# Two attention jobs of one head pair each become one job: scores of the lower and the upper 64 partitions alternate on TensorE

## The chip, the cores and the metric

The kernel runs on one core of one Trainium2 chip. The metric is device time in microseconds (us) of one launch; below it is better. TensorE (PE) does the matmuls, PEld is its weight load, VectorE is DVE, ScalarE is ACT, GpSimd is POOL, SyncE is SP.

## The reference

256 tokens of width 1024 go through four layers of a first block and two layers of a second one. A layer of the first block projects x to queries, keys and values, attends, adds an attention over 256 memory rows, projects out, normalises, and runs a gated feed-forward of width 2816. The attention differs by layer: 12 heads of 64 with a top-k mask picked by an index of 8 small heads (layers 0 and 3), 4 value heads that share three dilated score groups (layer 1), 12 plain causal heads (layer 2). A layer of the second block has three branches: differential attention (4 heads, two score maps of 64 each, the second subtracted), latent attention (8 heads whose scores contract over 96), and sliding-window attention (8 query heads on 2 key heads of 64).

```
logits = jnp.einsum('bqhd,bqkhd->bhqk', qb, ks) * scale      # d = 64
p = softmax(where(valid, logits, -inf))
o = jnp.einsum('bhqk,bqkhd->bqhd', p, vs)
```

## The kernel before

**Tiling.** The tokens are two tiles of 128, t = 0 and t = 1, each worked by a generator of its own (`stream(t)`). Nearly all of TensorE's work is in the weight matmuls of `gemm_part` (L375 to L377): a float32 weight is split into a high part H (ACT, L330) and a rest L (DVE, L331), and three matmuls with up to 512 columns make one product. These are called weight matmuls below, and six of them (two weight tiles) are a unit. The two streams take turns, a unit or so at a time.

**Jobs.** Attention is cut into stages that a queue per stream (`defer`, `job`, `tick`) releases one tick, that is one unit, after the other: stage a computes the scores and the softmax, stage b transposes the probabilities (`p_T`), stage c multiplies by the values (`pv`) and normalises. `attend_job` makes one such job from two heads; the jobs of a stream start one tick apart. Within an engine the recorded instructions are put in order by a list scheduler, so the code's order is not quite the engine's.

**Halves.** Transposed queries and keys hold two heads in one block of 128 partitions, one in the lower 64 (0 to 63) and one in the upper 64. A job takes two heads of the same half (`half_slice(e)`), so a group of four heads gives two jobs, e = 0 with the lower half and e = 1 with the upper half. The scores are plain float32 with 64 contraction rows; the profile shows each such matmul as two passes on PE. The heads of 96 rows use no halves.

**PSUM.** Scores, transposed probabilities and value products all take a bank from the pool tag "w" of their stream, which has two banks; the weight matmuls have two banks per stream of their own ("mm").

**Around it.** In `index_jobs`, `group(g)` is run for g = 0 to 3, two groups a tick, one for each half. `dilated_job(h)` computes three score groups of one head in one stage. `diff_job` computes the map of the lower half in one stage, that of the upper half in the next.

Of the kernel before, what the change touches and what calls it, by code (L numbers as in the profile page):

```python
# [14 lines left out]
AF = mybir.ActivationFunctionType  # L15
ALU = mybir.AluOpType
# [49 lines left out]
def tile_two_blocks(  # L66
# [277 lines left out]
    def job(t, *stages):  # L344
        at = max(now[t] + 1, started[t] + 1)
        started[t] = at
        for k, fn in enumerate(stages):
            defer(t, fn, at=at + k)
        return at + len(stages)
# [117 lines left out]
    def scores(t, qs, kss):  # L467
        s = psum([P, 2, 256], "w")
        for j, (q, ks) in enumerate(zip(qs, kss)):
            for n, k in enumerate(ks):  # L470
                w = k.shape[1]
                pe.matmul(s[:, j, n * P : n * P + w], q, k, start=True, stop=True)
        return s

    def soft_pair(t, nk, qs, kss, biases, sums, inits=None, mins=None):
        s = scores(t, qs, kss)
        sm = work_tile([P, 2, nk], "sm", 2)
        n = len(qs)
        mn = mins if mins is not None else small(2, "mn")
# [162 lines left out]
    def attend_job(t, nk, qs, kss, biases, vs, done, after=None, **kw):  # L642
        st = {}

        def a():
            st["sums"] = kw.get("sums", None) if "sums" in kw else small(2, "sums")
            st["sm"] = soft_pair(t, nk, qs, kss, biases() if callable(biases) else biases, st["sums"],
                                 inits=kw.get("inits"), mins=kw.get("mins"))

        def b():  # L650
            st["pt"] = p_T(st["sm"], len(qs), nk)

        def c():
            done(pv(st["pt"], len(qs), nk, vs), st["sums"])

        return job(t, a, b, c)

# [1 line left out]
    def block1(t):  # L659
# [6 lines left out]
        for i in range(DEPTH):  # L666
# [20 lines left out]
            def head_jobs(g, mk):  # L687
                for e in range(2):
                    hs = [g + e, g + 2 + e]
                    r = half_slice(e)  # L690
                    end = attend_job(
                        t, nk, [qT[r, h // 2, :] for h in hs], [[k[r, h // 2, :] for k in kTs] for h in hs], [mk, mk],
                        [[w[:, h * 64 : h * 64 + 64] for w in vs] for h in hs],
                        lambda o, sums, e=e: normalise(by_parity(mix, g, e), o, sums, 2, 64))
                return end

            def mem_jobs():
                def one(e):
                    r = half_slice(e)

                    def ks():
                        return [[mem_kv[i][r, 0, b, :]] for b in range(2)]

                    kv = mem_kv[i]
                    return attend_job(
                        t, 256, [qmT[r, b, :] for b in range(2)], ks(), None,
                        [[kv[:, 1, kt, c : c + 64] for kt in range(2)] for c in (64 * e, 128 + 64 * e)],
                        lambda o, sums: normalise(by_parity(mix[:, 768:1024], 0, e), o, sums, 2, 64))

                one(0)  # L710
                return one(1)

            def dilated_job(h):
                st = {}
                e = half_slice(h % 2)
                rsum = []

                def a():
                    sm = work_tile([P, 3, nk], "sm", 2)
                    mn = small(3, "mn3")  # L720
                    rsum.append(small(1, "rsum"))
                    pss = []
                    for grp in ((0, 1), (2,)):
                        bl = [(4 * g + h) // 2 for g in grp]
                        pss.append(scores(t, [qT[e, b, :] for b in bl], [[k[e, b, :] for k in kTs] for b in bl]))
                    for g in range(3):
                        vec.tensor_tensor_reduce(
                            out=sm[:, g], in0=pss[g // 2][:, g % 2, :nk], in1=shared["dil"][:, g, moff:], scale=1.0,
                            scalar=3.0e38 if g == 0 else mn[:, g - 1 : g],
                            op0=ALU.add, op1=ALU.min, accum_out=mn[:, g : g + 1])  # L730
                    act.activation(sm, sm, AF.Exp, bias=mn[:, 2:3], scale=-1.0, accum_out=rsum[0])
                    vec.tensor_tensor(out=sm[:, 1], in0=sm[:, 1], in1=sm[:, 2], op=ALU.add)
                    vec.tensor_tensor(out=sm[:, 0], in0=sm[:, 0], in1=sm[:, 1], op=ALU.add)
                    st["sm"] = sm

                def b():
                    st["pt"] = p_T(st["sm"], 1, nk)

                def c():
                    o = pv(st["pt"], 1, nk, [[w[:, h * 192 : h * 192 + 192] for w in vs]])  # L740
                    normalise(mix[:, h * 192 : h * 192 + 192].unsqueeze(1), o, rsum[0], 1, 192)

                return job(t, a, b, c)

            def index_jobs(wi):
                def group(g):
                    r = half_slice(g % 2)
                    hs = [4 * (g // 2) + g % 2, 4 * (g // 2) + 2 + g % 2]
                    s = scores(t, [qiT[r, h // 2, :] for h in hs], [[k[r, :] for k in kiTs]] * 2)
                    rl = work_tile([P, 2, nk], "sm", 2)  # L750
                    act.activation(rl, s[:, :, :nk], AF.Relu)
                    for e, h in enumerate(hs):
                        if h == 0:
                            vec.tensor_scalar(score[:, :nk], rl[:, e], wi[:, 0:1], None, op0=ALU.mult)
                        else:
                            vec.scalar_tensor_tensor(out=score[:, :nk], in0=rl[:, e], scalar=wi[:, h : h + 1],
                                                     in1=score[:, :nk], op0=ALU.mult, op1=ALU.add)
# [14 lines left out]
                for g in range(4):  # L772
                    defer(t, lambda g=g: group(g), after=IDX_WAIT + 1 + g // 2)
# [59 lines left out]
            if kind == 1:  # L833
                for s in range(2):
# [7 lines left out]
                    for h in (2 * s, 2 * s + 1):  # L842
                        end = dilated_job(h)
                    ends.append(end)
# [65 lines left out]
    def block2(t):  # L910
# [4 lines left out]
        for l in range(DEPTH_2):  # L915
# [86 lines left out]
            for h in range(0, 8, 2):  # L1002
                mk = causal[:, moff:]
                end_b = attend_job(
                    t, nk, [mqT[:96, h + e, :] for e in range(2)],
                    [[s[0][:96, h + e, :] for s in sh] for e in range(2)], [mk, mk],
                    [[s[1][:, (h + e) * 64 : (h + e) * 64 + 64] for s in sh] for e in range(2)],
                    lambda o, sums, h=h: normalise(ob[:, h * 64 : h * 64 + 128].rearrange("p (h d) -> p h d", d=64),
                                                   o, sums, 2, 64))
# [5 lines left out]
            def diff_job(h0):  # L1015
                st = {}

                def a(m):
                    r = slice(64 * m, 64 * m + 64)
                    if m == 0:  # L1020
                        st["bias"] = load_bias(t, h0)
                        st["sums"] = small(4, "sums4")
                    st[m] = soft_pair(t, nk, [aqT[r, h0 + e, :] for e in range(2)],
                                      [[s[2][r, h0 + e, :] for s in sh] for e in range(2)],
                                      [st["bias"][:, e, :] for e in range(2)], st["sums"][:, 2 * m : 2 * m + 2])
                    if m == 0:
                        return
# [18 lines left out]
                end = job(t, lambda: a(0), lambda: a(1), b, c)  # L1046
                started[t] += 1
                return end
# [13 lines left out]
            for g in range(2):  # L1062
# [6 lines left out]

                for e in range(2):  # L1070
# [3 lines left out]
                    end_c = attend_job(  # L1074
                        t, nk, [cqT[r, h // 2, :] for h in hs], [[s[4][r, g, :] for s in sh]] * 2,
                        lambda e=e, f=bias_of: f(e), [[s[5][:, g * 64 : g * 64 + 64] for s in sh]] * 2,
                        lambda o, sums, g=g, e=e: evac(by_parity(oc, 4 * g, e), o.rearrange("p (h d) -> p h d", d=64)),
                        sums=sums8[:, c : c + 2], inits=[nsink[:, l, h : h + 1] for h in hs], mins=mins8[:, c : c + 2])

            def finish_a():  # L1080
# [175 lines left out]
```

## Time and profile before

| | us |
|---|---|
| median of 3 runs | 1982.85 (1980.98 to 1984.48) |
| profiled execution, first to last instruction | 1982.1 |
| PE busy | 1940.6 |
| DVE busy | 1240.0 |
| ACT busy | 981.2 |

For the profiled execution no time is given but its span; it lies 0.75 us below the median. Busy PE is not the same as PE at its peak: matmuls are pipelined, and one that is shown with 0.39 us is followed by the next after 0.23 us. What a matmul costs is therefore read as the distance from its start to the next one's.

### The profile page before, as it was taken

How to read it: one execution, taken by the hardware profiler on the slowest of the kernel's cores; microseconds unless marked ns; L12 is line 12 of the kernel's file. 1: busy time of each engine (PE TensorE's matmuls, PEld its weight loads, DVE VectorE, ACT ScalarE, POOL GpSimd, SP SyncE). 2: the span in 40 equal slices, each digit the busy share in tenths (PEclk: the TensorE clock that was granted, in tenths of full speed). 3: DMA queues.
4: the chain of work that ended last, by engine and by line, in shares of the span. 5: the costliest groups of instructions: out<-in, count | busy, mean ns of one | idle time of the engine just before them, and what ended most of it. 6: DMA issues, size and time to landing. Idle time of an engine off the chain costs nothing. (4 is left out here: it accounts for less than half of the span.)

```text
span 1982.1 us, 27405 instructions
## 1 busy us (share of the span) xinstructions
PE 1940.6 (98%) x10013; PEld 1612.5 (81%) x10013; DVE 1240.0 (63%) x2148; ACT 981.2 (50%) x1650; POOL 211.0 (11%) x358
## 2 busy tenths in 40 slices
PE   7999999999999999999999999999999999999998
PEld 6888778888888878888877878887888887888886
DVE  5857555657665565765567576556666667566565
ACT  5654444444444455444445544445654456665453
POOL 4020000011000012000020200002121111111010
PEclk9999999999999999999999999999999999999999
DMA  6635666544665653565654356566446655445653
GB/s 197 187 99 158 209 184 199 182 136 131 209 182 174 198 169 107 158 192 155 211 178 134 105 161 191 159 208 175 119 145 179 186 177 168 120 141 149 188 184 106
DMA packets 198295, 327.55 MB, mean 165 GB/s; under 512 B 12914, under 2 KB 70838, under 8 KB 198160
## 3 DMA queue, kind: packets, MB, share of 16 engines
q1 hardware_dynamic: 191072, 306.03, 51.1%
q0 software_dynamic: 5312, 17.44, 2.8%
q10 hardware_dynamic: 1776, 2.33, 0.3%
q8 instruction: 79, 1.29, 0.3%
q14 instruction: 56, 0.46, 0.1%
HBM read 324.68 MB, written 3.43 MB: 166 GB/s over the span
## 5 line engine op out<-in xcount | busy, mean ns | idle before, releaser
L331 DVE TENSOR_TENSOR L<-raw,H 128x1024 fp32r<-128x1024 f32 (+3 forms) x616 | 727.7, 1182 | 452.3 <-ACT H L330 447.5
L330 ACT CAST H<-raw 128x1024 fp32r<-128x1024 f32 (+3 forms) x616 | 615.5, 1000 | 593.6 <-PE mm L377 457.8
L375 PE MATMUL mm<-H,xH 128*128 128x512 f32 (+3 forms) x1904 | 741.9, 391 | 1.9 <-ACT H L330 1.7
L377 PE MATMUL mm<-H,xL 128*128 128x512 f32 (+3 forms) x1904 | 717.7, 378 | 2.1 <-DVE xL L406 1.7
L376 PE MATMUL mm<-L,xH 128*128 128x512 f32 (+3 forms) x1904 | 716.0, 377 | 0.0
L375 PEld LDWEIGHTS mm<-H,xH 128*128 128x128 f32 x1904 | 358.6, 188 | 73.3 <-issue 5.0
L377 PEld LDWEIGHTS mm<-H,xL 128*128 128x128 f32 x1904 | 358.2, 188 | 71.3 <-DVE xL L406 3.1
L376 PEld LDWEIGHTS mm<-L,xH 128*128 128x128 f32 x1904 | 359.4, 189 | 55.9 <-DVE L L331 0.5
L375 PE MATMUL mm<-H,hH 128*128 128x512 f32 x352 | 137.6, 391 | 0.0
L376 PE MATMUL mm<-L,hH 128*128 128x512 f32 x352 | 137.2, 390 | 0.0
L377 PE MATMUL mm<-H,hL 128*128 128x512 f32 x352 | 137.0, 389 | 0.0
L423 POOL TENSOR_SCALAR pw_in<-mv 128x1 f32<-128x1 f32 x22 | 15.1, 690 | 822.1 <-DVE mv L432 822.0
L489 ACT ACTIVATE sm<-sm,mn 128x128 f32<-128x128 f32 (+1 forms) x136 | 60.9, 449 | 42.2 <-DVE mn L485 41.9
L398 PE MATMUL w<-cst,nat 128*128 128x128 f32 (+1 forms) x436 | 69.9, 276 | 11.3 <-DVE nat L896 6.2
L377 PEld LDWEIGHTS mm<-H,hL 128*128 128x128 f32 x352 | 66.1, 188 | 13.7
L375 PEld LDWEIGHTS mm<-H,hH 128*128 128x128 f32 x352 | 66.1, 188 | 13.1
L376 PEld LDWEIGHTS mm<-L,hH 128*128 128x128 f32 x352 | 66.1, 188 | 13.1
L398 PEld LDWEIGHTS w<-cst,nat 128*128 128x128 f32 (+1 forms) x436 | 51.8, 139 | 29.4 <-DVE nat L896 9.6
L413 ACT CAST xH<-w 128x512 fp32r<-128x512 f32 (+1 forms) x64 | 33.4, 532 | 53.9 <-PE w L398 51.9
L217 POOL TENSOR_TENSOR rope<-nat,rc 128x128 f32<-128x128 f32 (+1 forms) x38 | 20.2, 532 | 326.8 <-ACT nat L624 286.5
L498 PE MATMUL w<-cst,sm 128*128 128x128 f32 x304 | 52.5, 276 | 0.4
L398 PE MATMUL w<-cst,x 128*128 128x128 f32 x192 | 31.3, 290 | 15.4 <-DVE x L461 5.3
(262 smaller groups left out, 2023.4 us busy)
## 6 DMA issues: line engine op xcount, KB each, us to landing
raw<-in_w_gate_up_dram SPq DMA_DIRECT2D x160, 512.0 KB, 3.7
raw<-in_w_in_dram SPq DMA_DIRECT2D x104, 512.0 KB, 3.6
raw<-in_w_down_dram SPq DMA_DIRECT2D x88, 512.0 KB, 4.4
raw<-in_w_out_dram SPq DMA_DIRECT2D x48, 512.0 KB, 3.5
raw<-in_w_in_a_dram SPq DMA_DIRECT2D x56, 256.0 KB, 3.0
raw<-in_w_in_a_dram SPq DMA_DIRECT2D x16, 512.0 KB, 5.1
raw<-in_w_mem_kv_dram SPq DMA_DIRECT2D x16, 512.0 KB, 4.1
raw<-in_w_gate_up_dram SPq DMA_DIRECT2D x32, 256.0 KB, 2.8
```

Of the source, the lines that this page charges most:

```text
L217: eng.tensor_tensor(out=t1, in0=v, in1=bc(c), op=ALU.mult)
L330: act.copy(h, raw)
L331: vec.tensor_tensor(out=lo, in0=raw, in1=h.bitcast(F32), op=ALU.subtract)
L375: pe.matmul(a, xh[:, kt, :], h[:, j, :], start=st, stop=False)
L376: pe.matmul(a, xh[:, kt, :], lo[:, j, :], start=False, stop=False)
L377: pe.matmul(a, xl[:, kt, :], h[:, j, :], start=False, stop=en)
L398: pe.transpose(tr[:width, j, :], src(j), ident)
L413: act.copy(h, tr[:, :n, :])
L423: pool.tensor_scalar(v[:, :n], src, eps, None, op0=ALU.add)
L489: act.activation(sm[:, j, :], src, AF.Exp, bias=mn[:, j : j + 1], scale=-1.0, accum_out=sums[:, j : j + 1])
L498: pe.transpose(tr[:, j * nkt + kt, :], sm[:, j, kt * P : (kt + 1) * P], ident)
```

## The change

`attend_job` takes any number of sides. A job of two sides runs the scores of both in stage a, with the matmuls of the two sides alternating (lower, upper, lower, upper), each side into its own bank; stage b transposes both sides, and the value products of the sides follow in two further stages. With `span=2` the next job starts two ticks later, so a pair takes as many ticks as two jobs did. The head groups, the memory heads, the sliding-window groups and the differential maps are paired in this way; an index `group` now holds both halves; `dilated_job` takes two heads, one of each half, and computes the first two score groups in one stage and the third in the next. The latent heads go through the same code with one side. `small(2, "mn")` and `small(2, "sums")` get four buffers where they had two.

```
-    def scores(t, qs, kss):
-        s = psum([P, 2, 256], "w")
-        for j, (q, ks) in enumerate(zip(qs, kss)):
-            for n, k in enumerate(ks):
-                w = k.shape[1]
-                pe.matmul(s[:, j, n * P : n * P + w], q, k, start=True, stop=True)
-        return s
-
-    def soft_pair(t, nk, qs, kss, biases, sums, inits=None, mins=None):
-        s = scores(t, qs, kss)
+    def scores(t, *sides):
+        made = [psum([P, 2, 256], "w") for _ in sides]
+        for j in range(len(sides[0][0])):
+            for n in range(len(sides[0][1][j])):
+                for s, (qs, kss) in zip(made, sides):
+                    k = kss[j][n]
+                    pe.matmul(s[:, j, n * P : n * P + k.shape[1]], qs[j], k, start=True, stop=True)
+        return made
+
+    def softmax_of(t, s, n, nk, biases, sums, inits=None, mins=None):
         sm = work_tile([P, 2, nk], "sm", 2)
-        n = len(qs)
-        mn = mins if mins is not None else small(2, "mn")
+        mn = mins if mins is not None else small(2, "mn", bufs=4)
...
-    def attend_job(t, nk, qs, kss, biases, vs, done, after=None, **kw):
-        st = {}
+    def attend_job(t, nk, *sides):
+        st = [{} for _ in sides]
+        n = len(sides[0]["q"])
 
         def a():
-            st["sums"] = kw.get("sums", None) if "sums" in kw else small(2, "sums")
-            st["sm"] = soft_pair(t, nk, qs, kss, biases() if callable(biases) else biases, st["sums"],
-                                 inits=kw.get("inits"), mins=kw.get("mins"))
+            made = scores(t, *[(d["q"], d["k"]) for d in sides])
+            for x, d, s in zip(st, sides, made):
+                x["sums"] = d["sums"] if "sums" in d else small(2, "sums", bufs=4)
+                bias = d.get("bias")
+                x["sm"] = softmax_of(t, s, n, nk, bias() if callable(bias) else bias, x["sums"],
+                                     inits=d.get("inits"), mins=d.get("mins"))
 
         def b():
-            st["pt"] = p_T(st["sm"], len(qs), nk)
-
-        def c():
-            done(pv(st["pt"], len(qs), nk, vs), st["sums"])
-
-        return job(t, a, b, c)
...
+            for x in st:
+                x["pt"] = p_T(x["sm"], n, nk)
+
+        def c(i):
+            sides[i]["done"](pv(st[i]["pt"], n, nk, sides[i]["v"]), st[i]["sums"])
+
+        return job(t, a, b, *[lambda i=i: c(i) for i in range(len(sides))], span=len(sides))
...
             def head_jobs(g, mk):
+                sides = []
                 for e in range(2):
                     hs = [g + e, g + 2 + e]
                     r = half_slice(e)
...
+                return attend_job(t, nk, *sides)
...
+                return job(t, a0, a1, b, c, span=2)
...
-                for g in range(4):
-                    defer(t, lambda g=g: group(g), after=IDX_WAIT + 1 + g // 2)
+                for g in range(2):
+                    defer(t, lambda g=g: group(g), after=IDX_WAIT + 1 + g)
```

What TensorE runs changes as the following rows show, in the order in which the instructions stand on the engine. First TensorE in the first head group of layer 0. L472 (L473 after the change) are scores, L375 to L377 weight matmuls, L498 and L497 the transposes of `p_T`, L509 and L508 the value products. Before, `w_1223` are scores of stream 0, lower half, and `w_1253` scores of stream 1, upper half.

```order
L472 MATMUL w_1223<-b1_0_120 128x128 x2
L375 MATMUL mm_1134<-H_1082,xH1_153 128x512
L376 MATMUL mm_1134<-L_1083,xH1_153 128x512
L377 MATMUL mm_1134<-H_1082,xL1_154 128x512
L375 MATMUL mm_1134<-H_1082,xH1_153 128x512
L376 MATMUL mm_1134<-L_1083,xH1_153 128x512
L377 MATMUL mm_1134<-H_1082,xL1_154 128x512
L498 MATMUL w_1245<-cst_83,sm_1210 128x128 x4
L472 MATMUL w_1253<-b1_0_120,b1_1_169 128x128
L472 MATMUL w_1253<-b1_1_169 128x128
L472 MATMUL w_1253<-b1_0_120,b1_1_169 128x128
L472 MATMUL w_1253<-b1_1_169 128x128
```

After, `w_1204` (lower half) and `w_1205` (upper half) are the two sides of one job of stream 1.

```order
L377 MATMUL mm_1134<-H_1056,xL1_154 128x512
L473 MATMUL w_1204<-b1_0_120,b1_1_169 128x128
L473 MATMUL w_1205<-b1_0_120,b1_1_169 128x128
L473 MATMUL w_1204<-b1_1_169 128x128
L473 MATMUL w_1205<-b1_1_169 128x128
L473 MATMUL w_1204<-b1_0_120,b1_1_169 128x128
L473 MATMUL w_1205<-b1_0_120,b1_1_169 128x128
L473 MATMUL w_1204<-b1_1_169 128x128
L473 MATMUL w_1205<-b1_1_169 128x128
L375 MATMUL mm_1157<-H_1194,xH0_104 128x512
L376 MATMUL mm_1157<-L_1195,xH0_104 128x512
L377 MATMUL mm_1157<-H_1194,xL0_105 128x512
```

The lower and the upper half now stand in one run and alternate; the run of the upper half that stood behind the transposes is gone.

Second, TensorE a little later in layer 0: the memory heads' value products and the next head group of stream 1. Before, one half's scores come after the transposes:

```order
L509 MATMUL w_1461<-mkv_841,PT_1425 128x64 x4
L498 MATMUL w_1469<-cst_83,sm_1431 128x128 x4
L472 MATMUL w_1477<-b1_0_120,b1_1_169 128x128
L472 MATMUL w_1477<-b1_1_169 128x128
L472 MATMUL w_1477<-b1_0_120,b1_1_169 128x128
L472 MATMUL w_1477<-b1_1_169 128x128
L375 MATMUL mm_1398<-H_1451,xH0_1384 128x512
L376 MATMUL mm_1398<-L_1452,xH0_1384 128x512
```

Now both halves come behind half of a value product, and the upper one (`w_1487`) waits for the bank of that product, `w_1478`, to be read by DVE:

```order
L508 MATMUL w_1478<-mkv_841,PT_1444 128x64 x2
L473 MATMUL w_1486<-b1_0_120,b1_1_169 128x128
L473 MATMUL w_1486<-b1_1_169 128x128
L473 MATMUL w_1486<-b1_0_120,b1_1_169 128x128
L473 MATMUL w_1486<-b1_1_169 128x128
L375 MATMUL mm_1417<-H_1468,xH0_1403 128x512
L473 MATMUL w_1487<-b1_0_120,b1_1_169 128x128
L473 MATMUL w_1487<-b1_1_169 128x128
L473 MATMUL w_1487<-b1_0_120,b1_1_169 128x128
L473 MATMUL w_1487<-b1_1_169 128x128
L376 MATMUL mm_1417<-L_1469,xH0_1403 128x512
```

The scheduler kept the four matmuls of the lower half together and set a weight matmul between them and those of the upper half, so that two runs remain here.

Third, TensorE in layer 3, where index scores of stream 0 stand, `w_9276` for the lower half and, before, `w_9283` for the upper half:

```order
L376 MATMUL mm_9195<-L_9261,xH0_8950 128x512
L377 MATMUL mm_9195<-H_9260,xL0_8951 128x512
L472 MATMUL w_9276<-b1_0_8970,b2_0_8971 128x128 x2
L472 MATMUL w_9283<-b1_0_8970,b2_0_8971 128x128 x2
L375 MATMUL mm_9165<-H_9147,xH1_9047 128x328
L376 MATMUL mm_9165<-L_9148,xH1_9047 128x328
```

and after, with `w_9277` for the upper half:

```order
L377 MATMUL mm_9195<-H_9260,xL0_8951 128x512
L473 MATMUL w_9276<-b1_0_8970,b2_0_8971 128x128
L473 MATMUL w_9277<-b1_0_8970,b2_0_8971 128x128
L473 MATMUL w_9276<-b1_0_8970,b2_0_8971 128x128
L473 MATMUL w_9277<-b1_0_8970,b2_0_8971 128x128
L375 MATMUL mm_9165<-H_9147,xH1_9047 128x328
```

Both halves stood in one run already, two matmuls of one and then two of the other; now they alternate.

Over the whole program the scores with 64 rows stand in 114 runs before and in 73 after (a run is what stands between two other matmuls on PE). Of the 144 score matmuls of 128 columns that belong to the upper half, and the 16 of 256 columns:

| where the upper half's matmuls stand after the change | 128 columns | 256 columns |
|---|---|---|
| index heads | 24 | 0 |
| in a run, strictly alternating | 75 | 12 |
| in a run, two or three of one half and then of the other | 22 | 4 |
| in a run of their own, or beside a lower one in another run | 23 | 0 |

## Rows read from the trace of the kernel before

**Rows 1.** The page: busy time of each engine, and the granted clock in 40 slices.

```profile
PE 1940.6 (98%) x10013; PEld 1612.5 (81%) x10013; DVE 1240.0 (63%) x2148; ACT 981.2 (50%) x1650; POOL 211.0 (11%) x358
...
PEclk9999999999999999999999999999999999999999
```

**Rows 2.** Waits of PE, whole span: us in total, times, longest; first and near-last row.

```profile
PE w L398 <- DVE nat L896: 6.2, 6, 1.8
...
PE w L472 <- DVE b L393: 0.2, 1, 0.2
```

**Rows 3.** Score matmuls (L472): ns min/median/max, first and last start, forms.

```profile
L472 PE MATMUL w<-b,b x192: 272/272/373, 41.6 to 1146.0; 64*128 64x128 f32 x192
...
L472 PE MATMUL w<-b x192: 272/272/373, 76.9 to 1146.2; 64*128 64x128 f32 x192
...
L472 PE MATMUL w<-m x192: 272/272/377, 1397.2 to 1802.2; 64*128 64x128 f32 x128, 96*128 96x128 f32 x64
...
L472 PE MATMUL w<-m,m x96: 272/272/378, 1411.2 to 1801.9; 64*128 64x128 f32 x64, 96*128 96x128 f32 x32
...
L472 PE MATMUL w<-mkv,b x64: 376/376/480, 86.9 to 1081.1; 64*128 64x256 f32 x64
```

**Rows 4.** Timeline of PE around a run of 4 passes: start us, us.

```profile
1413.85 0.40 PE L377 MATMUL mm<-H,xL 128*128 128x512 f32 x1
1414.18 0.71 PE L472 MATMUL w<-m 64*128 64x128 f32 x4
1414.82 0.50 PE L375 MATMUL mm<-H,xH 128*128 128x512 f32 x1
1415.15 0.39 PE L376 MATMUL mm<-L,xH 128*128 128x512 f32 x1
1415.38 0.39 PE L377 MATMUL mm<-H,xL 128*128 128x512 f32 x1
```

**Rows 5.** Timeline of PE around a run of 8 passes, all of one half.

```profile
105.38 0.48 PE L472 MATMUL w<-b,b 64*128 64x128 f32 x2
...
106.46 0.50 PE L375 MATMUL mm<-H,xH 128*128 128x512 f32 x1
```

**Rows 6.** Timeline of PE, two runs of index scores, both halves in each.

```profile
1043.33 0.72 PE L472 MATMUL w<-b,b 64*128 64x128 f32 x8
1043.98 0.42 PE L375 MATMUL mm<-H,xH 128*128 128x328 f32 x1
...
50.96 1.71 PE L472 MATMUL w<-b,b 64*128 64x128 f32 x16
52.60 0.39 PE L375 MATMUL mm<-H,xH 128*128 128x256 f32 x1
```

**Rows 7.** Timeline of PE, a run of memory scores, 256 columns.

```profile
127.07 1.13 PE L472 MATMUL w<-mkv,b 64*128 64x256 f32 x4
128.13 0.66 PE L398 MATMUL w<-cst,nat 128*128 128x128 f32 x4
```

**Rows 8.** Timeline of DVE, ACT and PE behind the run of rows 5.

```profile
106.57 0.42 DVE L485 CUSTOM_DVE_ANT_0 sm<-w,b 128x256 f32<-128x256 f32 x1 [1.64 <-PE w L472]
...
107.03 0.51 ACT L489 ACTIVATE sm<-sm,mn 128x256 f32<-128x256 f32 x1 [0.51 <-DVE mn L485]
...
107.26 1.22 DVE L331 TENSOR_TENSOR L<-raw,H 128x1024 fp32r<-128x1024 f32 x1
...
107.55 0.49 ACT L489 ACTIVATE sm<-sm,mn 128x256 f32<-128x256 f32 x1
...
110.18 0.60 PE L498 MATMUL w<-cst,sm 128*128 128x128 f32 x4
110.38 1.04 ACT L330 CAST H<-raw 128x1024 fp32r<-128x1024 f32 x1 [0.31 <-PE mm L377]
```

**Rows 9.** Busy us of each engine in two stretches of attention.

```profile
41.00:175.00 134.00, 131.68 (x810) 110.78 (x810) 91.35 (x235) 76.46 (x163) 17.16 (x33) 1.00 0.44 135
...
1390.00:1500.00 110.00, 109.15 (x656) 91.14 (x655) 70.81 (x211) 65.31 (x177) 20.52 (x32) 1.00 0.47 135
```

More of the change, by code (lines that the diff above doesn't have):

```diff
@@ L690, in head_jobs @@
                     r = half_slice(e)
[L691 to L695, printed above, removed]
+                    sides.append(dict(
+                        q=[qT[r, h // 2, :] for h in hs], k=[[k[r, h // 2, :] for k in kTs] for h in hs], bias=[mk, mk],
+                        v=[[w[:, h * 64 : h * 64 + 64] for w in vs] for h in hs],
+                        done=lambda o, sums, e=e: normalise(by_parity(mix, g, e), o, sums, 2, 64)))
@@ L697, in mem_jobs @@
+                return attend_job(t, nk, *sides)
             def mem_jobs():
-                def one(e):
+                kv = mem_kv[i]
+                sides = []
+                for e in range(2):
                     r = half_slice(e)
[L701 to L723, printed above, removed]
-                        bl = [(4 * g + h) // 2 for g in grp]
[L725 to L734, printed above, removed]
@@ L841, in block1 @@
                     started[t] = max(started[t], now[t] + QK_WAIT)
[L842 to L844 removed]
+                    ends.append(dilated_job(s))
             else:
@@ L1016, in diff_job, with a @@
                 st = {}
[L1018 to L1027, printed above, removed]
+                def a():
+                    bias = load_bias(t, h0)
+                    st["sums"] = small(4, "sums4")
+                    rows = [slice(64 * m, 64 * m + 64) for m in range(2)]
+                    made = scores(t, *[([aqT[r, h0 + e, :] for e in range(2)],
+                                        [[s[2][r, h0 + e, :] for s in sh] for e in range(2)]) for r in rows])
+                    for m in range(2):
+                        st[m] = softmax_of(t, made[m], 2, nk, [bias[:, e, :] for e in range(2)],
+                                           st["sums"][:, 2 * m : 2 * m + 2])
                     rc = small(4, "r4")
@@ L1044, in c @@
                     vec.tensor_copy(oa[:, h0 * P : h0 * P + 2 * P], o)
-                end = job(t, lambda: a(0), lambda: a(1), b, c)
-                started[t] += 1
-                return end
+                return job(t, a, b, c, span=2)
             for h0 in (0, 2):
@@ L1073, in block2 @@
                     c = 4 * g + 2 * e
[L1074 to L1078, printed above, removed]
+                    sides.append(dict(
+                        q=[cqT[r, h // 2, :] for h in hs], k=[[s[4][r, g, :] for s in sh]] * 2,
+                        bias=lambda e=e, f=bias_of: f(e), v=[[s[5][:, g * 64 : g * 64 + 64] for s in sh]] * 2,
+                        done=lambda o, sums, g=g, e=e: evac(by_parity(oc, 4 * g, e),
+                                                            o.rearrange("p (h d) -> p h d", d=64)),
+                        sums=sums8[:, c : c + 2], inits=[nsink[:, l, h : h + 1] for h in hs], mins=mins8[:, c : c + 2]))
+                end_c = attend_job(t, nk, *sides)
             def finish_a():
```

82 lines of the change are left out of this document (59 added, 23 removed).

## The prediction

> **What bounds the kernel now.** I read the page first: PE is busy 1940.6 of 1982.1 us, DVE 63%, ACT 50%, and the clock of PE is granted in full (the 2.4 GHz level) in every slice [rows 1]. Then PE's waits: seventeen rows that sum to about 36 us, nearly all at transposes behind a norm or at the start; at the score matmuls one row of 0.2 us, at the probabilities' transposes and the value products none [rows 2]. So PE's own work is the time, stage by stage, in attention too. A change pays here by what it takes from PE, as long as it brings no wait.
>
> Third, the timeline of PE, to price the scores. A weight matmul of 512 columns costs 0.23 us, start to start (1415.15 to 1415.38) [rows 4]. From the weight matmul before a run of 4 score passes (1413.85) to the second one after it (1415.15) are 1.30 us; two weight matmuls would be 0.46, so the run costs 0.84 [rows 4]. Inside a run, 4 passes take 0.64 to the next weight matmul (1414.18 to 1414.82) and 8 take 1.08 (105.38 to 106.46) [rows 4, 5]: four more cost 0.44, 0.11 each. 0.84 less 4 x 0.11 leaves **0.40 us for the run itself**: the start of the first pass comes late, and so do the first two weight matmuls behind it. A 256-column pass comes from 127.07 to 128.13, 1.06 for four, against 0.64 for four of 128: 0.105 more, 0.215 each [rows 4, 7].
>
> The whole of it: 576 passes of 128 columns and 64 of 256 [rows 3] in 114 runs: 114 x 0.40 + 576 x 0.11 + 64 x 0.215 = 45.6 + 63.4 + 13.8, about 123 us of PE.
>
> **What two halves in one run cost.** The trace of before shows this already, at the index heads. There two matmuls (four passes) of the lower half are followed by four passes of the upper half, in one run. These 8 passes take 1043.33 to 1043.98, 0.65 us [rows 6], just what 4 passes of one half take (0.64, [rows 4]). So passes of the two halves run side by side: a pair costs one pass, 0.11. The run of 16 (stream 1, eight of each half) takes 50.96 to 52.60, 1.64 [rows 6]; unpaired it would be 1.08 (105.38 to 106.46, [rows 5]) + 8 x 0.11 = 1.96, so only three pairs' worth was saved: what is eight passes apart meets only in part.
>
> One rule speaks against a full gain where a run holds two or three matmuls of one half and then the other. The Trainium skill ("TensorE: Matmul & The Clock Gate", "The mechanism" in Part 3) has matmuls start and end in program order. By it only the pair at the change of half would meet, 0.1 us a run, and my sum below would be some 2.4 us smaller; the run of 8 that took the time of 4 does not agree with it, since nearly all of its pairs must have met.
>
> **The change part by part.**
>
> Runs: 114 become 73, by the order. 41 x 0.40 = **16.4 us** saved. Where a run goes that stood behind transposes instead of a weight matmul I take the same price.
>
> Pairs of 128 columns: 75 upper matmuls alternate strictly, 150 passes x 0.11 = 16.5. 22 stand in a run behind two or three of the lower half, partly with a wait of their own ahead: 44 passes, from nothing to 4.8; I take half, 2.4, since [rows 6] shows both a full and a partial case. 23 stand apart: nothing. Together **18.9**.
>
> Pairs of 256 columns: no row shows a pair of this size. Below, nothing; above, a full pair at 0.215. The smaller pairs are nearest and were full, so I take 0.215 for the 12 that alternate (24 passes, 5.2) and half for the 4 that don't (0.9): **6.1**.
>
> Index heads: in stream 1 four runs of 16 passes at 1.64 [rows 6] become runs of eight pairs at 1.08 [rows 5]: 4 x 0.56 = **2.2**. In stream 0 one run is at its floor already; the other three I leave.
>
> Sum of what PE loses: 16.4 + 18.9 + 6.1 + 2.2 = **43.6 us**.
>
> What is added. First, **a longer chain from scores to transposes.** Both sides' scores now end together, and stage b takes both. Behind one side today (stream 1): minimum-and-bias on DVE from 106.57, two of them to 107.26, 0.35 each; exponentials on ACT from 107.03, 0.52 apart, the second at 107.55 and done at about 108.04; the transposes on PE at 110.18 [rows 8]. That is 2.14 us of slack. With two sides the four exponentials end at 107.03 + 4 x 0.52 = 109.11, and 1.07 us remain, just a weight cast of ACT (1.04, [rows 8]). The transposes stand behind about as many weight matmuls as before, so in the usual place the chain is covered; where a cast and a subtraction of DVE both fall into it, or fewer weight matmuls stand between, PE waits some tenths. What queues behind a PE wait is everything, the weight matmuls of both streams.
>
> Second, **both banks of "w" at once.** The upper half's scores can wait for DVE to read the bank of the value product or of the transposes just before. The scheduler put weight matmuls in between at some places, and at others the lower half's scores cover it.
>
> There are 46 paired jobs (18 head groups, 8 memory, 8 differential, 8 sliding, 4 dilated). Below, no wait at all, as almost none shows today [rows 2]; above, 0.3 us in each, the size of the shortfall where a cast (1.04) and a 0.35 step both come in (1.39 - 1.07), 14 us. I take 0.1 each, **4.6 us**, nearer to nothing because today's waits are.
>
> At no cost: the buffers of `mn` and `sums` (small tiles); the order of `load_bias` on POOL's queue, with as many loads as before, ahead of their scores by the same stage; the tick count of a pair, 2 + 3 as before, so the end of attention comes at the same unit. Weight transfers and casts must come 2% faster: DVE is busy 91 of 134 and 71 of 110 us in attention, ACT 76 and 65, the DMA engines 0.44 and 0.47 [rows 9]. If that cover went, PE would wait at L375 for H.
>
> **Sum.** 1982.1 - 43.6 + 4.6 = 1943.1. The median of the runs lies 0.75 us above the profiled span: 1943.9, say **1944 us**, 1.9% faster. With every pair of the non-index heads full (240 passes, 26.4, and 6.9 for the large ones) and no wait it would be 16.4 + 26.4 + 6.9 + 2.2 = 51.9, 1931. With half of the strict pairs' gain, half of 16.5 + 5.2, 10.9, nothing from the other pairs or the index, and 14 us of waits: 16.4 + 10.9 - 14 = 13, 1970.
>
> **The rivals.**
>
> *The softmax chain takes over.* DVE and ACT have no less to do and PE gets less time to cover them. By the stretches of attention this is no matter of throughput (DVE 68%, ACT 57 to 59%, [rows 9]), but the chain of one pair can be late at each job: at 0.4 to 0.5 us in 46 jobs, some 21 us, the time is 1982.9 - 43.6 + 21 = 1960. For it: the slack falls from 2.14 to 1.07. Against: three units mostly stand between, and PE hardly waits today. The Trainium skill ("TensorEngine Tiling (Array Packing)", "PSUM Bottleneck") says just this, that packing speeds up TensorE and not the reading of PSUM, which may become the bound; the trace bears it out so far as the slack halves, not as a bound.
>
> *The merge holds, the pairs do not.* If passes of the halves meet only where the queue happens to run ahead, the runs still go: 16.4 - 4.6 = 11.8, 1971. Against: the run of 8 in the time of 4. That the change does nothing at all is excluded by the order.
>
> *Slower.* The upper half's wait for its bank decides. All 43.6 us are gone when it costs 43.6 / 46 = 0.95 us a job: that is, when in each job DVE takes a weight subtraction (1.22 us, [rows 8]) between the value product and its normalising while PE has nothing left to issue. At 1.2 us in every job: 1982.9 + 55 - 43.6 = 1995. For it: PE takes its queue in order, and there are just two banks. Against: before, the same two banks turned over as often per tick, and score matmuls waited 0.2 us in all.
>
> *All pairs full, no wait:* 1931 to 1935.
>
> **How the numbers follow.** My forecast, 1936 to 1954: 0.64. All full: 0.06. The chain, 1954 to 1968: 0.15. No pairing, 1968 to 1979: 0.10, of which 0.02 within 0.2%. Slower or even: 0.05. A difference of 0.2% (4 us) is about what a measurement of this kernel can tell from none. Range for 8 in 10: 1931 to 1970. Faster 0.94, same 0.03, slower 0.03.
>
> **What would show it.** In the changed profile: PE busy less by about 40 us; runs of 8 passes over both halves in stream 0's head groups at about 0.65 us and of 16 at about 1.1; memory runs of 8 passes at about 1.1; the score lines' weight-to-weight distances otherwise as now; PE waits for ACT's exponentials or for L515 and L484 (DVE) of a few us in all. The forecast is wrong if paired passes start 0.11 us apart instead of nearly together, if PE waits at transposes or upper scores sum to over 15 us, or if L375 begins to wait for H.

## The result, and the profile after

The changed kernel takes 1950.17 us, median of 4 runs (1947.05 to 1952.12), against 1982.49 (1980.98 to 1984.48, 4 runs) for the kernel before on the same chip: a ratio of 0.9829, 95% interval 0.9814 to 0.9844. It is 1.7% faster. The forecast was 1944 in a range of 1931 to 1970; the result lies 6 us above the point.

The profiled execution is the fastest of the four: its span is 1945.2 us, 36.9 less than before's 1982.1; the others span 1947.8 to 1950.4. The page of the changed kernel, busy time of each engine and the granted clock of PE:

```profile
PE 1902.3 (98%) x10013; PEld 1584.4 (81%) x10013; DVE 1242.0 (64%) x2152; ACT 972.2 (50%) x1646; POOL 204.3 (10%) x358
...
PEclk9999999999999999999999999999999999999999
```

PE is busy 38.3 us less and still 98% of the span; DVE and ACT have about the same work as before, in a shorter time. PE is still the bound.

Waits of PE in the changed kernel, over the whole span (us in total, times, longest):

```profile
PE w L398 <- POOL nat L220: 4.4, 9, 1.3
...
PE w L398 <- DVE nat L908: 4.1, 4, 2.5
...
PE w L497 <- ACT sm L488: 2.5, 3, 1.9
...
PE mm L375 <- ACT H L330: 1.6, 1, 1.6
...
PE w L473 <- DVE b L393: 1.3, 1, 1.3
...
PE mm L376 <- DVE L L331: 0.6, 1, 0.6
...
PE w L473 <- DVE mn L725: 0.4, 1, 0.4
```

All rows together sum to 36.7 us; those of before to 35.7. What is new beside [rows 2] is the wait of the probabilities' transposes (L497) for ACT's exponentials, 1.7 us at the scores instead of 0.2, and 0.6 us of a weight matmul (L376) for its L. Most rows at transposes behind a norm have become smaller in this profile, and so the sum is nearly the same; in that of e0 below, the same kernel, the row of L908 is 7.1 us.

The timeline of PE around the run that was [rows 5] before: start us, us, line, operation, count.

```profile
103.15 0.39 PE L376 MATMUL mm<-L,xH 128*128 128x512 f32 x1
103.37 0.40 PE L377 MATMUL mm<-H,xL 128*128 128x512 f32 x1
103.70 0.49 PE L473 MATMUL w<-b,b 64*128 64x128 f32 x4
104.02 0.39 PE L473 MATMUL w<-b 64*128 64x128 f32 x4
104.25 0.39 PE L473 MATMUL w<-b,b 64*128 64x128 f32 x4
104.47 0.39 PE L473 MATMUL w<-b 64*128 64x128 f32 x4
104.79 0.50 PE L375 MATMUL mm<-H,xH 128*128 128x512 f32 x1
105.12 0.39 PE L376 MATMUL mm<-L,xH 128*128 128x512 f32 x1
```

Sixteen passes, eight of each half, take 103.70 to 104.79, 1.09 us, against 1.08 for eight of one half in [rows 5]. The pairs meet in full, and the upper half costs nothing more. A run of eight passes, four of each half, takes 0.64 us where it alternates, the price of four passes of one half in [rows 4]:

```profile
106.38 0.71 PE L473 MATMUL w<-b 64*128 64x128 f32 x8
107.02 0.50 PE L375 MATMUL mm<-H,xH 128*128 128x512 f32 x1
```

A sum over the whole trace says what the score runs cost PE. For each run of scores with 64 rows I take the distance from its first start to the next other matmul, add what its first pass comes late behind the matmul before it, and what the second weight matmul behind it comes late. Before, 114 runs cost 120.0 us; after, 73 runs cost 79.9. That is 40.1 us less. The waits at the scores stand in these sums, 0.2 us before and 1.7 after, so that the runs without their waits cost 41.6 us less. PE's other waits fell by 0.5 us and a clock drop cost 1.7 us (below); 40.1 + 0.5 - 1.7 gives 38.9, and the span lost 36.9. The 2.0 us between them have no row of their own: the distances between PE's other matmuls are a little longer.

### The profile page after: what moved, and what is told of

Same layout as the page of the kernel before. It is cut to its first block, busy times and chain, and to the rows that moved or that the text cites. A ratio compares the mean times of both kernels' runs of the same rounds, so it can differ in the third digit from the quotient of the medians.

```text
span 1945.2 us, 27394 instructions
## 1 busy us (share of the span) xinstructions
PE 1902.3 (98%) x10013; PEld 1584.4 (81%) x10013; DVE 1242.0 (64%) x2152; ACT 972.2 (50%) x1646; POOL 204.3 (10%) x358
## 5 line engine op out<-in xcount | busy, mean ns | idle before, releaser
L375 PE MATMUL mm<-H,xH 128*128 128x512 f32 (+3 forms) x1904 | 740.8, 390 | 1.9 <-ACT H L330 1.6
L377 PE MATMUL mm<-H,xL 128*128 128x512 f32 (+3 forms) x1904 | 719.8, 379 | 2.1 <-DVE xL L406 1.7
L376 PE MATMUL mm<-L,xH 128*128 128x512 f32 (+3 forms) x1904 | 718.6, 378 | 0.6 <-DVE L L331 0.6
L377 PEld LDWEIGHTS mm<-H,xL 128*128 128x128 f32 x1904 | 358.4, 188 | 69.4 <-DVE xL L406 3.2
L375 PEld LDWEIGHTS mm<-H,xH 128*128 128x128 f32 x1904 | 359.1, 189 | 67.7 <-ACT xH L413 3.3
L376 PEld LDWEIGHTS mm<-L,xH 128*128 128x128 f32 x1904 | 359.5, 189 | 57.9 <-DVE L L331 1.5
L375 PE MATMUL mm<-H,hH 128*128 128x512 f32 x352 | 137.5, 391 | 0.0
L376 PE MATMUL mm<-L,hH 128*128 128x512 f32 x352 | 137.3, 390 | 0.0
L377 PE MATMUL mm<-H,hL 128*128 128x512 f32 x352 | 137.0, 389 | 0.0
L488 ACT ACTIVATE sm<-sm,mn 128x128 f32<-128x128 f32 (+1 forms) x136 | 60.4, 446 | 40.5 <-DVE mn L484 40.2
L377 PEld LDWEIGHTS mm<-H,hL 128*128 128x128 f32 x352 | 66.1, 188 | 13.8
L375 PEld LDWEIGHTS mm<-H,hH 128*128 128x128 f32 x352 | 66.2, 188 | 13.2
L376 PEld LDWEIGHTS mm<-L,hH 128*128 128x128 f32 x352 | 66.2, 188 | 12.8
L413 ACT CAST xH<-w 128x512 fp32r<-128x512 f32 (+1 forms) x64 | 33.0, 531 | 43.3 <-PE w L398 41.6
L497 PE MATMUL w<-cst,sm 128*128 128x128 f32 x304 | 48.6, 278 | 2.7 <-ACT sm L488 2.5
L497 PEld LDWEIGHTS w<-cst,sm 128*128 128x128 f32 x304 | 36.6, 144 | 12.1 <-ACT sm L488 4.7
```

The source lines that it names most:

```text
L375: pe.matmul(a, xh[:, kt, :], h[:, j, :], start=st, stop=False)
L376: pe.matmul(a, xh[:, kt, :], lo[:, j, :], start=False, stop=False)
L377: pe.matmul(a, xl[:, kt, :], h[:, j, :], start=False, stop=en)
L413: act.copy(h, tr[:, :n, :])
L488: act.activation(sm[:, j, :], src, AF.Exp, bias=mn[:, j : j + 1], scale=-1.0, accum_out=sums[:, j : j + 1])
L497: pe.transpose(tr[:, j * nkt + kt, :], sm[:, j, kt * P : (kt + 1) * P], ident)
```

## The experiments

The sum over the score runs (waits at the scores included), the waits of PE and the times of all kernels. The ratio is to runs of the kernel before on the same chip.

| kernel | score runs | their cost, us | PE waits, us | median, us | ratio (95%) |
|---|---|---|---|---|---|
| before | 114 | 120.0 | 35.7 | 1982.49 | 1 |
| changed | 73 | 79.9 | 36.7 | 1950.17 | 0.9829 (0.9814 to 0.9844) |
| e0, changed once more | 73 | 80.2 | 38.6 | 1950.26 | 0.9827 (0.9814 to 0.9841) |
| e1, one half only | 73 | 109.1 | 31.7 | 1969.44 | 0.9936 (0.9916 to 0.9957) |
| e2, halves one after the other | 70 | 85.7 | 37.0 | 1955.1 | 0.9857 (0.9843 to 0.987) |
| e3, layer 3's memory later | 73 | 80.0 | 37.0 | 1949.65 | 0.9828 (0.9814 to 0.9841) |
| e5, scores released first | 71 | 75.9 | 38.3 | 1944.71 | 0.9805 (0.9791 to 0.982) |
| e5b, the same again | 71 | 75.7 | 39.0 | 1945.23 | 0.9807 (0.9791 to 0.9823) |
| e6, transposes a stage later | 73 | 82.3 | 39.2 | 1950.37 | 0.9835 (0.982 to 0.9849) |
| e8, memory heads apart | 81 | 88.8 | 35.9 | 1955.35 | 0.9854 (0.9838 to 0.9871) |
| e9, e5 and later differential jobs | 67 | 71.1 | 38.7 | 1944.75 | 0.9804 (0.979 to 0.9818) |
| e9b, the same again | 67 | 71.0 | 39.3 | 1944.0 | 0.9797 (0.9783 to 0.981) |

**e0: the changed kernel, as it is.** Expected:

> The changed kernel again, unedited, for an interval and a second profile. Expected 1947 to 1952 us; score runs (start to next matmul, with late neighbours) about 80 us of PE against 120 before. If the 1.2 GHz stretch of 3.4 us at 1047 us of the first profile comes from the 1.9 us wait before it, it is there again at the same place; if it is chance, it is elsewhere or gone.

1950.26, as before. Its profiled span is 1949.2, 4 us more than the first one, with the same score runs (80.2) and 1.9 us more of waits: so much does one profiled execution differ from another. The clock drop of the first profile is there again, behind the same wait (last section).

**e1: both sides use the lower half.** The jobs, the stages, the two banks and the order stay; only the pairing of the halves is gone. The scores of the upper heads are replaced by ones from the lower half's rows.

```
-            half_slice = lambda e: slice(64 * e, 64 * e + 64)
+            half_slice = lambda e: slice(0, 64)
...
-                    rows = [slice(64 * m, 64 * m + 64) for m in range(2)]
+                    rows = [slice(0, 64) for m in range(2)]
...
-                    r = slice(64 * e, 64 * e + 64)
+                    r = slice(0, 64)
```

> Both sides of every job read the lower 64 partitions, so that no two passes can run side by side; the merged jobs, their order and all else stay (the upper heads' scores are replaced by the lower heads'). Theory (pairs and merged runs each pay): the pairs' part is lost, 576 x 0.111 + 64 x 0.216 of passes and 76 runs at 0.40 make 108 us of scores, 28 more than now, so about 1978 us, still 4 to 8 below the kernel before... and some 2 us may hide in waits. Rival (merged runs alone pay): 1950 to 1955 us.

1969.44, between the theory's 1978 and the rival's 1950 to 1955. The same run as above, in the timeline of PE of this kernel:

```profile
104.55 0.71 PE L473 MATMUL w<-b,b 64*128 64x128 f32 x4
105.10 0.61 PE L473 MATMUL w<-b 64*128 64x128 f32 x4
105.55 0.61 PE L473 MATMUL w<-b,b 64*128 64x128 f32 x4
106.00 0.61 PE L473 MATMUL w<-b 64*128 64x128 f32 x4
106.53 0.50 PE L375 MATMUL mm<-H,xH 128*128 128x512 f32 x1
```

1.98 us for sixteen passes instead of 1.09, though the banks alternate as in the changed kernel. So it is the two halves that meet; alternating banks alone pair nothing. Merging by itself brings about 14.5 us of time (1983.97, the median of before in this comparison, to 1969.44), and the pairs about 19; as e1 also loses the pairs that the index heads had before (2.5 us on PE, next section), merging is worth somewhat more than that and the new pairs somewhat less. On PE the pairs are worth more: the score runs cost 109.1 here against 80.2 in e0, 28.9 us. The difference comes back in part as waits. This kernel's rows of waits at the same places:

```profile
PE w L398 <- DVE nat L908: 4.2, 4, 2.1
PE w L398 <- DVE x L461: 3.8, 7, 0.7
PE w L398 <- POOL nat L220: 3.1, 8, 0.6
...
PE w L473 <- DVE b L393: 1.3, 1, 1.3
```

There is no row at L497. Its waits sum to 31.7, those of e0 to 38.6 and of the changed kernel's first profile to 36.7: the pairs bring 5 to 7 us of waits with them, at the transposes behind ACT and behind the norms. Of the 10 that are missing (28.9 less 18.9, the difference of the two profiled spans), 3 to 4 us have no row of their own.

**e2: all passes of the lower half first, then the upper.**

```
-        for j in range(len(sides[0][0])):
-            for n in range(len(sides[0][1][j])):
-                for s, (qs, kss) in zip(made, sides):
+        for s, (qs, kss) in zip(made, sides):
+            for j in range(len(sides[0][0])):
+                for n in range(len(sides[0][1][j])):
```

> Both halves in one job, but all scores of the lower half are recorded before those of the upper one; nothing else. Theory (passes of the other half run ahead by some four passes): runs of 2 + 2 matmuls still take about 0.65 us, runs of 4 + 4 about 1.6 instead of 1.09, some 18 runs, memory runs about 1.5 instead of 1.06: 10 to 14 us slower, about 1962 us. Rival (passes start in program order, so one pair meets in a run): most pairs are lost, 20 to 25 us slower, about 1973 us. Rival (order in a run is no matter): 1950 us.

1955.1, 5 us more than the changed kernel, where the theory had 10 to 14. The scores' sum rose by 5.5 us (85.7 against 80.2); as the waits in it fell from 1.8 us to 0.2, the runs alone cost 7.1 us more. The same run in the timeline of PE:

```profile
103.90 0.48 PE L473 MATMUL w<-b,b 64*128 64x128 f32 x2
104.23 0.38 PE L473 MATMUL w<-b 64*128 64x128 f32 x2
104.45 0.49 PE L473 MATMUL w<-b,b 64*128 64x128 f32 x4
104.68 0.49 PE L473 MATMUL w<-b 64*128 64x128 f32 x4
105.01 0.38 PE L473 MATMUL w<-b,b 64*128 64x128 f32 x2
105.23 0.38 PE L473 MATMUL w<-b 64*128 64x128 f32 x2
105.54 0.50 PE L375 MATMUL mm<-H,xH 128*128 128x512 f32 x1
```

In program order the eight lower passes come first and the eight upper ones behind them. The trace, which is in order of time, shows two groups of two passes alone, two groups of four in the time of two, and two of two alone: the upper half started four passes early, beside the lower half's fifth. The run takes 1.64 us, the same as [rows 6], and so do all fifteen runs of this kind. Of the runs of two matmuls of each half most were full here, 15 of 21 at 0.65 us as in [rows 6], and six of eight memory runs at 1.07, where the theory had 1.5. So in these runs a pass of one half overtakes about four of the other, and no more. Grouping costs mainly in stream 1, where a half has up to eight passes.

**e3: one empty stage before the transposes of one job**, the memory heads of layer 3 in stream 0, where the changed kernel's longest new wait stands (last section). Stage b of that job comes one tick later.

> The memory job of layer 3, stream 0, has an empty tick between its scores and its transposes; nothing else. Theory (its two reductions on DVE queue behind the top-k selection, PE waits 1.9 us and then runs 3.4 us at 1.2 GHz): both go, 3 to 4 us faster than the changed kernel, about 1946 us. Rival (the wait moves to the next consumer): same as the changed kernel within 1 us.

1949.65, no change that can be told. The long wait there is shorter (the longest at L497 is 1.2 instead of 1.9), but two clock drops came at other places, in layer 0's feed-forward. What was removed at one place was not gained.

**e5: scores ahead of the value products of the same tick.** In the queue of a stream, stage a of a two-sided job gets the first place in its tick.

```
-    def defer(t, fn, after=1, at=None):
+    def defer(t, fn, after=1, at=None, early=0):
...
-        heapq.heappush(queues[t], (now[t] + after if at is None else at, count[0], fn))
+        heapq.heappush(queues[t], (now[t] + after if at is None else at, count[0] - early, fn))
...
-            defer(t, fn, at=at + k)
+            defer(t, fn, at=at + k, early=1000000 if k == 0 and span == 2 else 0)
```

> The scores of a two-sided job are released ahead of the value products that fall into the same tick, so that neither half has to wait for the bank of a value product. By the order there are 71 runs instead of 73; the four lower and four upper runs of 4 passes that stood apart become alternating ones, the four memory and stream-1 runs that held two or three of one half and then of the other alternate too (one more pair of 8-pass runs stands apart). Theory (every run costs about 0.4 us and every pair that meets saves 0.11, or 0.215 at 256 columns, and nothing comes back): 4 x 0.84 for the runs that go, 4 x 0.38 and 2 x 0.45 for the pairs that then meet, less 1.28 for the pair that goes apart, 4.5 us less than the changed kernel: 1945.5. Rival (what PE gains at these places comes back as a wait behind DVE and ACT, since the softmax of the pair is no earlier than PE's other work lets it): 1950, as the changed kernel.

1944.71, near the theory's 1945.5. The scores' cost fell by 4.0 us on PE (79.9 to 75.9), 4.5 expected, and the time by 5.5; this run was on another chip than those of the changed kernel, and by the ratios to before (0.9805 against 0.9827 and 0.9829) it is 4 to 5. The value product had held the bank that the upper half waits for, so the scheduler had put the halves apart or grouped them; with the scores first, all eight memory jobs alternate.

**e6: every two-sided job of `attend_job` with one empty stage between scores and transposes.**

```
-        return job(t, a, b, *[lambda i=i: c(i) for i in range(len(sides))], span=len(sides))
+        return job(t, a, lambda: None, b, *[lambda i=i: c(i) for i in range(len(sides))], span=len(sides))
```

> Every two-sided job gets one empty stage between its scores and its transposes, so that the chain of four exponentials has a tick more. By the order the runs stay 73, with fewer alternating ones: about 1.6 us more of scores. Theory (the longer chain is what the changed kernel loses against its sum): PE's waits for ACT at the transposes of the probabilities, 2.5 us, go, and the clock drop behind the longest of them, 3.41 us at half the clock, worth 1.7 us, with them: 1950 + 1.6 - 4.2, about 1947.5. Rival (the chain is covered nearly everywhere and what a delay removes at one place shows up at another): 1951 to 1953.

1950.37, between the two. The waits at L497 fall to one row, `PE w L497 <- ACT sm L488: 1.2, 1, 1.2`, and the profiled run has no clock drop until its end; but the scores cost 2.4 us more, as fewer alternate, and PE waits 39.2 us in all. So the longer chain may cost about 2 us, and a later stage b lose as much in the scores' order; this is argued from the 2.4 us and not shown, as the runs of this kernel alone spread over 4 us (1949.4 to 1953.7).

**e8: the memory heads as two one-sided jobs again, in all layers.**

```
-                return attend_job(t, 256, *sides)
+                attend_job(t, 256, sides[0])
+                return attend_job(t, 256, sides[1])
```

> The memory heads of all four layers go back to two one-sided jobs; the rest stays as changed. By the order 81 runs instead of 73. Theory (a run costs 0.4 us and a pair of 256-column passes that meets saves 0.215): 8 jobs x (0.4 + 4 x 0.215) = 10.1 more, less 0.9 for the two jobs that met only in part, 9.2 us: 1959.5. Rival (the pair of 256-column scores gives its gain back, since their four exponentials and two minima come late): no more than 1955, with PE's waits for ACT at the transposes and the clock drop of layer 3 gone.

1955.35, 5.1 us more, though the scores cost 8.9 more on PE (9.2 expected): between the theories, close to the rival's 1955. Paired memory scores gain 8.9 on PE and give back about 4, partly as waits: these are 0.8 to 2.7 us fewer here than in the two profiles of the changed kernel, and the longest at L497 is 1.1.

**e9: e5, and the differential jobs of stream 1 one tick later each.** In e5 their halves still stood apart, since the upper half's bank was that of a value product of the tick before.

```
+            started[t] += t
             for h0 in (0, 2):
                 end_a = diff_job(h0)
+                started[t] += t
```

> The kernel with the scores released first, and in stream 1 of the second block each differential job starts one tick later, so that the bank of the value product before it has been read. By the order the four pairs of runs of 4 lower and 4 upper matmuls that still stood apart become four alternating runs of 16 passes: 67 runs instead of 71. Theory (a run costs 0.4 us, a met pair of passes saves 0.11): 4 x (0.4 + 8 x 0.11) = 5.1 us less than with the scores first: 1939.6. Rival (the later end of attention or of its softmax costs what the pairs give): 1944 to 1946.

1944.75, the same as e5, where 1939.6 was expected. The runs are as planned, 67, and cost 4.8 us less on PE. The two kernels had not run side by side, so both ran again in one comparison:

> The kernel with the scores released first once more, beside the next one on one chip. Both theories: 1943 to 1946.

> The kernel with the later differential jobs once more, on the chip of the run before it. Theory (the 4.8 us that its scores lost on PE are real, and the first comparison was blurred by the spread from run to run): 4 to 5 us under the kernel with the scores first. Rival (what these runs save comes back as waits and clock drops): within 1.5 us of it.

1945.23 and 1944.0. Rows of the page, busy time, first of e5b, then of e9b:

```profile
PE 1902.0 (98%) x10013; PEld 1580.6 (81%) x10013; DVE 1240.8 (64%) x2152; ACT 971.0 (50%) x1646; POOL 205.6 (11%) x358
```

```profile
PE 1897.3 (98%) x10013; PEld 1577.6 (81%) x10013; DVE 1240.7 (64%) x2150; ACT 972.6 (50%) x1648; POOL 205.8 (11%) x358
```

PE's busy time fell by 4.7, the medians by 0 and 1.2; over nine runs each they are 1945.0 and 1944.3. At the same weight matmul, counted from the start, the profile of e9b is ahead of e5b's by 1.3 us more after each of the two layers' differential jobs, where the scores alone give 2.4. So 1.1 of it is lost on the spot, in pieces of a few tenths at transposes and value products; where the rest of the medians' difference goes, the spread of the runs (1942.7 to 1949.7 and 1941.4 to 1945.4) hides. e5 and e9 are both faster than the changed kernel; e9 over e5 is not shown.

## Why the prediction was right, and by how much it was off

- **What bounds the kernel.** Right: PE is busy 98% of a shorter span. Its work in the score runs went down by 41.6 us without their waits, and the span by 36.9.
- **The pairs.** Right in mechanism and size. Alternating passes of the halves run side by side: 15 of 17 alternating runs of eight passes take 0.65 us, nine of ten of sixteen take 1.09, and at 256 columns eight take 1.07 (1039.89 to 1040.96, below), which no row of before had shown. In sum: e1 against e0, 28.9 us, and 0.5 more without the waits at the scores (1.8 in e0, 1.3 in e1), less what e1 itself loses at the index heads, where before had paired some (four runs of 1.98 instead of 1.64, and four of 1.08 instead of 0.65, 0.77, 0.89 and 0.91, 2.5): 26.9. The terms 18.9 + 6.1 + 2.2 were 27.2. That they are this close is partly luck, since the half that was taken for the grouped runs was a choice. It came out about right: in the changed kernel four grouped runs of sixteen passes take 1.42 to 1.52 us, between 1.09 and 1.98, and the two grouped memory runs 1.51 and 1.55, between 1.06 and 1.92 (e1). e2 shows that groups of four passes can meet in full; the changed kernel's two grouped memory runs, whose upper half comes behind a value product, take 1.06 with the scores released first (e5).
- **The rule that was weighed**, matmuls starting and ending in program order (the Trainium skill, "TensorE: Matmul & The Clock Gate", "The mechanism" in Part 3), does not hold between the two halves: in e2 the upper half's first pass starts four passes ahead of its place, and most grouped runs of eight passes are full.
- **The runs: the term that was mis-sized.** 41 x 0.40 = 16.4 was the forecast. e1 against before measures 120.0 - 109.1 = 10.9. In e1's sum stand 1.1 us more of waits at the scores and the 2.5 of the index heads; without them it is 14.5, or 0.35 a run, 1.9 us less than forecast. The price was read at a run between weight matmuls [rows 4] and taken for those behind transposes too. Most of the runs that went had stood there: 73 of the 114 runs stood beside a transpose or a value product, and 15 of the 73 that remain. But by the same distances in the trace of before a run between two of these costs only about 0.05 us less than one between weight matmuls, so this is a small part of the 1.9; what makes up the rest is not shown.
- **The longer chain and the banks.** 4.6 us were forecast in 46 jobs. Measured: 2.5 at L497, and 1.7 at the scores (0.2 before), together 4.0 more, but not spread over the jobs: three waits and two. So the size was met by chance; a tenth in each job was not the mechanism. The longest, 1.9, stands behind DVE's top-k selection (last section); the 1.3 at the scores comes with the merge alone, since e1 has that row too. Shorter waits elsewhere, mostly behind norms, took 3 us off again in the first profile and 1 in that of e0.
- **Not foreseen:** a drop of the granted clock, 1.7 us in the profile, which before had in other executions too (below).
- **The rest of the miss** is the distance from the profiled span to the median: 0.75 was taken, and here it is 5.0 (1950.17 - 1945.2), since the profiled execution was the fastest of four. Against e0's span, 1949.2, the forecast sum of 1943.1 is 6.1 too low: 2.2 in the score runs (41.4 without their waits, instead of 43.6) and 1.7 for one clock drop, less 1.7 since its waits grew by 2.9 and not by 4.6; for the 3.9 that remain I have no row.
- **The rivals.** The softmax chain did not take over: 2.5 us at L497, not 21. The pairs hold: e1 is the kernel without them, and 1969.44 lies near the 1971 that was worked out for that case. The upper half's wait for its bank is no more than a part of the 1.7 us at the scores, not 0.95 us a job. The weight matmuls' wait for H stayed at one row of 1.6 us (1.7 before); the wait of 0.6 us for L is new.

## What to carry to other kernels

Matmuls with 64 rows pair on TensorE when one uses the lower and the next the upper half, and each writes a bank of its own, as all of them did here (one bank for both was not tried); price the pair from a run in which both halves already stand together, if the trace has one. A run of such matmuls between others costs something by itself, so merge runs, but read that price apart for each neighbour. And once PE's own work shrinks, ask what the freed bank, the longer softmax chain and another engine's queue do: of 29 us that the pairs took from PE, 19 reached the time, and putting the scores ahead of the value products brought 4 to 5 more.

## What the runs showed of the hardware that was not expected

**Passes of the other half overtake.** e2's run, above: the upper half's first pass starts beside the lower half's fifth of eight, four ahead of its place; the run takes 1.64 us where strict order would take 1.98 less one pair, and full pairing 1.09.

**A wait behind another engine's queue, and a clock drop.** In layer 3 of the changed kernel, stream 0, the paired memory scores are followed by this (timeline; DVE, ACT and PE; the bracket is the idle time before an instruction, and what ended it):

```profile
1039.89 1.14 PE L473 MATMUL w<-mkv,b 64*128 64x256 f32 x8
...
1040.48 1.22 DVE L331 TENSOR_TENSOR L<-raw,H 128x1024 fp32r<-128x1024 f32 x1
...
1040.96 0.39 PE L375 MATMUL mm<-H,xH 128*128 128x256 f32 x1
...
1041.61 0.42 DVE L779 MAX8 m<-b 128x8 f32<-128x256 f32 x1
...
1041.95 1.21 DVE L331 TENSOR_TENSOR L<-raw,H 128x1024 fp32r<-128x1024 f32 x1
...
1043.47 0.68 DVE L480 TENSOR_REDUCE mn<-w 128x2 f32<-128x512 f32 x1
...
1044.19 0.47 ACT L488 ACTIVATE sm<-w,mn 128x256 f32<-128x256 f32 x1 [4.25 <-DVE mn L480]
1044.41 0.67 DVE L480 TENSOR_REDUCE mn<-w 128x2 f32<-128x512 f32 x1
...
1045.26 0.66 PE L497 MATMUL w<-cst,sm 128*128 128x128 f32 x4 [1.94 <-ACT sm L488]
```

The scores are done at 1040.96, but the minimum that the exponentials need starts on DVE only at 1043.47, since weight subtractions and the steps of the top-k selection (L779 and L780) stand ahead of it. The row names ACT; the late one is DVE. Before, the same two memory jobs stood a tick apart. Then the clock, in windows of 2 us (busy time of PE, PEld, DVE, ACT and POOL, granted clock, DMA share, GB/s):

```profile
1042.00:1044.00 2.00, 1.33 (x6) 0.75 (x4) 2.00 (x5) 0.00 (x0) 0.00 (x0) 1.00 0.58 154
1044.00:1046.00 2.00, 0.74 (x7) 0.74 (x8) 1.97 (x8) 1.81 (x5) 0.00 (x0) 1.00 0.96 288
1046.00:1048.00 2.00, 2.00 (x13) 1.54 (x11) 1.93 (x4) 2.00 (x7) 0.00 (x0) 0.67 0.25 87
1048.00:1050.00 2.00, 2.00 (x8) 1.61 (x7) 1.73 (x5) 0.49 (x1) 0.00 (x0) 0.50 0.62 176
1050.00:1052.00 2.00, 2.00 (x17) 1.91 (x17) 1.91 (x6) 0.29 (x2) 0.00 (x0) 0.98 0.40 109
```

PE idles 0.67 and 1.26 us in two windows; after it has resumed, the granted clock falls to the lower of its two levels (0.50 in the row, 1.2 GHz). Three windows lose 0.33 x 2 + 0.50 x 2 + 0.02 x 2 = 1.7 us of full clock, about as much again as the wait. The profile of before has no such drop until the end of its span. Nearly every changed kernel has one or two, and not always at the same place: e0 at 1048.8, behind the same wait as here, e1 at 239.9, e3 at 235.3 and 320.6, each behind a wait of PE of about 2 us; e6, where the wait here is 1.2, has none. But the longest wait of the changed kernel's profile, 2.50 us at 232.95 (the row of L908 above), is followed by no drop, nor is e5's wait of 1.94 at the place shown here, nor are waits of 1.83 and 1.71 us at 238.94 and 253.74 in the profile of before. And the drops are not shown to come with the change: the profile of before has a mean granted clock of 1.000, but 11 of the 33 executions of before that ran beside e0 to e9b have 0.998 or 0.997, as low as e0's profile with its one drop (0.998). What decides it these runs do not settle.
